# Residual of the last norm moved into the gate passes; factors for W2's first rows through the ring of f's blocks

## The chip, the cores and the metric

One core of a Trainium2 chip runs the whole layer in one launch. The metric is device time in microseconds, the median of several runs. Engines: PE (matmuls), DVE (vector), ACT (scalar, with activation functions), POOL and SP; SP, ACT and POOL also issue DMAs. Each engine runs its own instructions strictly in order.

## The reference

One layer of a transformer trunk in float32, with 512 tokens and 2048 features: two kinds of attention on one input projection, an output product, a layer norm, then a feed-forward part and a gated embedding, and a second layer norm:

```
mix = concat(RMSNorm_A(A), RMSNorm_B(B)) @ w_o
h   = LN1(alpha*x + mix)
ff  = square(relu(h @ w1)) @ w2                  # w1 2048 x 8192, w2 8192 x 2048
ple = (p @ w_ple) * sigmoid(h @ w_ple_gate)      # w_ple 256 x 2048, gate 2048 x 2048
out = LN2(alpha*h + ff + ple)                    # alpha = 2 ** 0.25
```

LN1 is `(x - mean) * rstd * ln1_g + ln1_b`, row by row. The term `alpha*h + ple` is what this text calls the residual.

## The kernel before

**Products.** From the output product on, every product is a call of `strassen`: two by two blocks, seven products in place of eight. A pass has 28 steps `(p, k)`, product p and row block k. A step loads a 128x1024 block of weights or makes a sum of such blocks on DVE, splits it into two parts for PE's fast float32 mode (`w_split`: `wh` on ACT, line 87, `wl = w - wh` on DVE, line 88; three buffers of each), and gives PE 12 matmuls of 128x512: `wh` with both parts of the activation's factor, `wl` with the first. Three chains of PSUM banks, `a`, `b` and `c`, hold the sums. After the last row block of a product, `read` copies or adds the chain into a tile of the ring `c` (line 682 on ACT, line 684 on DVE). `after` calls the consumer of a finished quarter two steps later.

**Order of the passes.** One pass of `w_o` by this method; two of the gate (c = 0, 1); eight of W1 (n = 0 to 7), each giving 1024 features of f; eight of W2 (m = 0 to 3, c = 0, 1). Between `w_o` and the gate, `norm_rows` normalises z, and `turned` (line 695) stores it to `z_d`, transposes it on PE, lets ACT apply LN1's gain and bias (line 708), and stores the result, h turned by features, to `h_d`. So `h_d` holds h itself, and `z_d` holds z without gain and bias.

**Factors.** The activation's factors, a high and a low part `s1h`/`s1l` to `s7h`/`s7l` for each half g, are made by `put` (ACT line 433, DVE line 434). For W2, `f_factors` loads blocks of f's sums from `s_d` (tile `qs`, line 589) and splits them, each at a step of the pass before, or, if its product is in `LATE`, at a step of the pass itself.

**Residual before.** In each gate pass `gated` (line 759) takes a sigmoid in place and stores it to `g_d`. In each W1 pass `residual(n % 2, n // 2)` has three parts, hung on steps 6, 10 and 13: `load` brings z, the sigmoid, the embedding's product and LN1's gain and bias, 512 KB each, through SP's queue; `scaled` (lines 778, 781) and `summed` (lines 786, 787) make the residual on DVE, and POOL's queue stores it back to `z_d`. W2's passes add to `z_d`, and the last ones read it.

**Rings.** `w_tile` gives buffers by tag, in turn: `r` 4 (weight blocks), `q` 2 (`wq`, and in f's factors `qs`), `k` 4, `c` 3, `g` 4 (the residual's tiles, h's blocks `qh`, and in W2 the weight blocks `wg` where `hold` is set). A tile that asks for a buffer waits until the former owner's last reader is done. A load that waits for its buffer holds the queue of the engine that issues it.

**Order of the instructions.** The program text gives priorities; the framework's scheduler settles the order on each engine when the kernel is built, and may move an instruction ahead of another one of its engine. What follows on the order is read from the built programs.

Of the kernel before, what the change touches and what calls it, by code (L numbers as in the profile page):

```python
# [11 lines left out]
F32 = mybir.dt.float32  # L12
# [26 lines left out]
def block_kernel(ctx: ExitStack, tc: tile.TileContext, xT, xn, pT, positions, w_in, w_o, w_gate, w_ple,  # L39
# [356 lines left out]

    g_d = dr.tile([2, 4, P, 2, S], F32, name="g_d")


    def embed(g, p, bank, pair_of):  # L400
# [180 lines left out]
    def f_factors(m, sg):  # L581


        at = {False: {}, True: {}}
        for p in range(1, 8):
            for g in range(2):
                def step(p=p, g=g):
                    x = block("qs", "q")
                    nc.sync.dma_start(x, s_d[2 * m + g, p - 1])
                    put(sg[g], p, x)  # L590
                late = p in LATE
                at[late].setdefault(LATE[p][g] if late else STEPS.index((p, 2 * g + 1)) + 2, []).append(step)
        return at
# [101 lines left out]
    def turned(th, n):  # L695

        z, g = zs[th, n], n % 2
        nc.gpsimd.dma_start(z_d[th, n], z)
        i = 2 * th + n // 2
# [58 lines left out]
    for c in range(2):  # L758
        def gated(th, nh, g, c=c):
            nc.scalar.activation(g, g, AF.Sigmoid)  # L760
            nc.scalar.dma_start(g_d[th, 2 * c + nh], g)
        strassen(lambda k, q, c=c: w_gate[c, q, k], sh, quarters(gated), between=mid if c == 0 else {},
                 steps=FIRST5 if c == 0 else None)

    def residual(th, n):

        t = {}

        def load():
            for name, d in (("zn", z_d), ("sg", g_d), ("pl", ple_d)):  # L770
                t[name] = pair(name, "g")
                nc.sync.dma_start(t[name], d[th, n])
            t["gb"] = pair("gb", "g")
            nc.sync.dma_start(t["gb"], bass.AP(tensor=lnb.tensor, offset=lnb.offset + n * S,
                                               ap=[[0, P], [D, 2], [1, S]]))

        def scaled():
            nc.vector.tensor_tensor(t["sg"], t["sg"], t["pl"], op=ALU.mult)
            for i in range(2):
                z = t["zn"][:, i]  # L780
                nc.vector.scalar_tensor_tensor(z, z, ALPHA, t["gb"][:, 0], op0=ALU.mult, op1=ALU.mult)

        def summed():
            for i in range(2):
                z = t["zn"][:, i]
                nc.vector.scalar_tensor_tensor(z, t["gb"][:, 1], ALPHA, z, op0=ALU.mult, op1=ALU.add)
            nc.vector.tensor_tensor(t["zn"], t["zn"], t["sg"], op=ALU.add)
            nc.gpsimd.dma_start(z_d[th, n], t["zn"])

        return load, scaled, summed  # L790

# [3 lines left out]
    for n in range(NFC):  # L795
        f = {}
        mid = dict(at[False]) if n == NFC - 1 else {}
        for i, step in zip((6, 10, 13), residual(n % 2, n // 2)):
            mid[i] = mid.get(i, []) + [step]

        def squared(th, nh, x, n=n, f=f):
# [16 lines left out]
            if (th, nh) == (0, 0):  # L818
# [5 lines left out]
                keep(3, f[0, 1])  # L824
        strassen(lambda k, q, n=n: w1[n, q, k], sh, quarters(squared), between=mid)

# [3 lines left out]
    def last_sum(c):  # L830
# [5 lines left out]
        def read(p, b):  # L836
# [11 lines left out]
            if c == 1 and p == 5:  # L848
                for n in range(2):
                    gb.append([])  # L850
                    for i in range(2):
                        x = s_tile("gb", ("s5h", "s5l")[i], (P, 1024))
                        off = lnb.offset + (2 + i) * D + n * 1024
                        nc.gpsimd.dma_start(x, bass.AP(tensor=lnb.tensor, offset=off, ap=[[0, P], [1, 1024]]))
                        gb[n].append(x)
# [144 lines left out]
```

## Time and profile before

| | us |
|---|---|
| median of 3 runs | 2275.27 (2273.86 to 2276.92) |
| profiled execution | 2280.34 |
| its span | 2278.6 |
| PE busy | 2166.3 (95%) |
| DVE busy | 1636.1 (72%) |
| ACT busy | 1060.7 (47%) |

Busy time adds up instructions of one engine; a busy PE says nothing on its clock, which the views of stretches give beside it as PEclk, 1.00 for full speed (2.4 GHz), and which falls to the lower level (1.2 GHz) for a while after idle time. The passes stand in this order in the span: `w_o` to about 704 us, the norm's turning to about 762, gate to 926 or so, W1 to about 1620, W2 to the end. In the views a wait is named by who ended it. DMA names read target<-source, so `gb<-in_lnb` is the load of LN1's gain and bias.

### The profile page before, as it was taken

How to read it: one execution, taken by the hardware profiler on the slowest of the kernel's cores; microseconds unless marked ns; L12 is line 12 of the kernel's file. 1: busy time of each engine (PE TensorE's matmuls, PEld its weight loads, DVE VectorE, ACT ScalarE, POOL GpSimd, SP SyncE). 2: the span in 40 equal slices, each digit the busy share in tenths (PEclk: the TensorE clock that was granted, in tenths of full speed). 3: DMA queues.
4: the chain of work that ended last, by engine and by line, in shares of the span. 5: the costliest groups of instructions: out<-in, count | busy, mean ns of one | idle time of the engine just before them, and what ended most of it. 6: DMA issues, size and time to landing. Idle time of an engine off the chain costs nothing.

```text
span 2278.6 us, 25699 instructions
## 1 busy us (share of the span) xinstructions
PE 2166.3 (95%) x9576; PEld 1752.2 (77%) x9576; DVE 1636.1 (72%) x1872; ACT 1060.7 (47%) x1287; POOL 115.1 (5%) x192
## 2 busy tenths in 40 slices
PE   8999999999997899999999999989999999999995
PEld 7888888877785688877778777776777787787784
DVE  7675655544878777776877877767767777777887
ACT  5454333343344554445445445455545555555331
POOL 0000000000001000000000000000011011011000
PEclk9999999999998999999999999999999999999998
DMA  6212322237566675566676676676778779679562
GB/s 228 75 65 84 116 72 82 78 113 261 167 211 234 241 244 196 169 229 205 221 239 208 219 238 204 220 257 228 247 208 261 195 196 290 178 209 291 181 242 102
DMA packets 133230, 438.79 MB, mean 193 GB/s; under 512 B 13776, under 2 KB 21984, under 8 KB 133104
## 3 DMA queue, kind: packets, MB, share of 16 engines
q1 hardware_dynamic: 98832, 316.45, 41.4%
q0 software_dynamic: 26336, 95.53, 14.6%
q10 hardware_dynamic: 7936, 25.17, 3.1%
q8 instruction: 75, 1.23, 0.2%
q14 instruction: 51, 0.42, 0.1%
HBM read 354.25 MB, written 82.84 MB: 192 GB/s over the span
## 4 chain that ended last, share of the span: by engine, by line
PE 66%; DMA 12%; issue 10%; DVE 10%; ACT 2%; POOL 0%; DVEq 0%; SPq 0%; ACTq 0%; POOLq 0%
PE a L666 8%; PE a L663 8%; PE a L665 8%; PE u L94 6%; PE u L96 6%; PE u L95 6%; DVE wl L88 4%; PE b L666 3%; PE b L663 3%; PE b L665 3%; DMA wr<-in_w 3%; PE c L666 3%; PE c L663 3%; PE c L665 3%; DMA s_d<-f 2%
## 5 line engine op out<-in xcount | busy, mean ns | idle before, releaser
L87 ACT ACTIVATE wh<-wr 128x1024 fp32r<-128x1024 f32 (+1 forms) x400 | 415.9, 1042 | 587.2 <-PE a L665 263.8
L88 DVE TENSOR_TENSOR wl<-wr,wh 128x1024 fp32r<-128x1024 f32 (+1 forms) x400 | 478.7, 1199 | 239.8 <-ACT wh L87 233.0
L87 ACT ACTIVATE wh<-wk 128x1024 fp32r<-128x1024 f32 x152 | 160.9, 1059 | 191.9 <-PE a L665 101.8
L94 PE MATMUL u<-xh,wh 128*128 128x512 f32 x576 | 227.4, 395 | 5.9 <-ACT xh L74 5.9
L96 PE MATMUL u<-xh,wl 128*128 128x512 f32 x576 | 225.7, 392 | 0.0
L88 DVE TENSOR_TENSOR wl<-wk,wh 128x1024 fp32r<-128x1024 f32 x152 | 185.1, 1221 | 56.4 <-ACT wh L87 56.3
L95 PE MATMUL u<-xl,wh 128*128 128x512 f32 x576 | 225.2, 391 | 0.0
L610 DVE TENSOR_TENSOR wk<-wr,wk 128x1024 f32<-128x1024 f32 x76 | 93.0, 1223 | 87.0 <-DMA wr<-in_w 78.0
L663 PE MATMUL b<-wh,s5h 128*128 128x512 f32 x304 | 122.4, 403 | 14.9 <-DVE c L684 8.4
L666 PE MATMUL a<-wl,s6h 128*128 128x512 f32 x304 | 122.0, 401 | 12.1 <-DVE wl L88 12.1
L94 PEld LDWEIGHTS u<-xh,wh 128*128 128x128 f32 x576 | 108.6, 188 | 27.6 <-ACT xh L74 5.9
L663 PE MATMUL a<-wh,s6h 128*128 128x512 f32 x304 | 121.7, 400 | 7.8 <-ACT ev L884 4.6
L96 PEld LDWEIGHTS u<-xh,wl 128*128 128x128 f32 x576 | 108.4, 188 | 22.8
L663 PE MATMUL a<-wh,s7h 128*128 128x512 f32 x304 | 120.6, 397 | 5.4 <-ACT wh L87 5.4
L95 PEld LDWEIGHTS u<-xl,wh 128*128 128x128 f32 x576 | 108.5, 188 | 22.3 <-DVE xl L75 0.4
L666 PE MATMUL b<-wl,s5h 128*128 128x512 f32 x304 | 122.5, 403 | 3.2 <-DVE wl L88 3.2
L665 PE MATMUL a<-wh,s1l 128*128 128x512 f32 x304 | 120.7, 397 | 4.7 <-DVE s1l L434 4.7
L666 PE MATMUL c<-wl,s2h 128*128 128x512 f32 x304 | 120.8, 397 | 3.7 <-DVE wl L88 3.6
L666 PE MATMUL a<-wl,s7h 128*128 128x512 f32 x304 | 120.5, 396 | 4.0 <-DVE wl L88 4.0
L666 PE MATMUL a<-wl,s1h 128*128 128x512 f32 x304 | 121.1, 398 | 2.0 <-DVE wl L88 2.0
L663 PE MATMUL a<-wh,s1h 128*128 128x512 f32 x304 | 121.2, 399 | 1.7 <-ACT wh L87 1.7
L663 PE MATMUL c<-wh,s2h 128*128 128x512 f32 x304 | 121.5, 400 | 0.3 <-ACT wh L87 0.3
(285 smaller groups left out, 4674.2 us busy)
## 6 DMA issues: line engine op xcount, KB each, us to landing
wr<-in_w SPq DMA_DIRECT2D x196, 512.0 KB, 4.4
wq<-in_w SPq DMA_DIRECT2D x72, 512.0 KB, 4.5
wr<-in_w_in SPq DMA_DIRECT2D x64, 512.0 KB, 3.8
wk<-in_w POOLq DMA_DIRECT2D x64, 512.0 KB, 5.5
qs<-s_d SPq DMA_DIRECT2D x56, 512.0 KB, 4.8
z_d<-ev POOLq DMA_DIRECT2D x42, 512.0 KB, 6.7
wr<-in_w_o SPq DMA_DIRECT2D x32, 512.0 KB, 4.3
s_d<-f POOLq DMA_DIRECT2D x32, 512.0 KB, 4.2
```

The lines of the kernel that those rows point to most:

```text
L87: nc.scalar.activation(hi, t, AF.Copy)
L88: nc.vector.tensor_tensor(lo, t, hi.bitcast(F32), op=ALU.subtract)
L94: nc.tensor.matmul(o, wh, ah, start=start, stop=False)
L95: nc.tensor.matmul(o, wh, al, start=False, stop=False)
L96: nc.tensor.matmul(o, wl, ah, start=False, stop=stop)
L610: nc.vector.tensor_tensor(t4[k], get(b21, k, 2, "r"), t2[k], op=ALU.subtract)
L663: nc.tensor.matmul(o, sh[:, i, x], wh[:, c], start=first and k == 0 and j == 0, stop=False, skip_group_check=skip)
L665: nc.tensor.matmul(o, sl[:, i, x], wh[:, c], start=False, stop=False, skip_group_check=skip)
L666: nc.tensor.matmul(o, sh[:, i, x], wl[:, c], start=False, stop=k == 3 and j == 1, skip_group_check=skip)
```

## The change

The residual is made in the gate passes. `gated` loads the embedding's product (`pl`) and a block of h turned by features (`hk`, from `h_d`) through ACT's queue into the ring `g`, multiplies sigmoid and product on DVE, transposes h back with eight transposes on PE, adds alpha times that out of PSUM on DVE (two instructions), and stores the sum to `z_d` from ACT's queue. With this `turned` no longer stores z, `residual` and `g_d` are gone, and W1's passes hold nothing of it. LN1's gain and bias are no longer among the inputs `lnb`. Second, the `qs` of W2's first rows (m = 0) take their buffers from `g` in place of `q`, and for the second half two of them, products 3 and 7, are split in the first W2 pass (steps 4 and 6) in place of the last W1 pass (steps 20 and 21).

```diff
--- before.py
+++ after.py
@@ -394,9 +394,6 @@
     hd.scores(q, k)
 
 
-    g_d = dr.tile([2, 4, P, 2, S], F32, name="g_d")
-
-
     def embed(g, p, bank, pair_of):
         wh, wl = w_split(w_load(w_ple[g], "r"))
         for th in range(2):
@@ -585,11 +582,12 @@
         for p in range(1, 8):
             for g in range(2):
                 def step(p=p, g=g):
-                    x = block("qs", "q")
+                    x = block("qs", "q" if m else "g")
                     nc.sync.dma_start(x, s_d[2 * m + g, p - 1])
                     put(sg[g], p, x)
-                late = p in LATE
-                at[late].setdefault(LATE[p][g] if late else STEPS.index((p, 2 * g + 1)) + 2, []).append(step)
+                plan = LATE if m or g == 0 else {**LATE, 3: (3, 4), 7: (3, 6)}
+                late = p in plan
+                at[late].setdefault(plan[p][g] if late else STEPS.index((p, 2 * g + 1)) + 2, []).append(step)
         return at
 
     def strassen(src, sg, read, hold=False, between={}, steps=None):
@@ -695,7 +693,6 @@
     def turned(th, n):
 
         z, g = zs[th, n], n % 2
-        nc.gpsimd.dma_start(z_d[th, n], z)
         i = 2 * th + n // 2
         ha[g, i] = x = s_tile("ha", {0: "s4h", 1: "s4l", 2: "s7h", 3: "s7l"}[i])
         for b0 in (0, 2):
@@ -757,47 +754,27 @@
     mid = {3 + 2 * n: [f] for n, f in enumerate(steps[0] + steps[1])}
     for c in range(2):
         def gated(th, nh, g, c=c):
+            n = 2 * c + nh
+            e = pair("pl", "g")
+            nc.scalar.dma_start(e, ple_d[th, n])
+            hk = block("hk")
+            nc.scalar.dma_start(hk, h_d[n % 2, 2 * th + n // 2])
             nc.scalar.activation(g, g, AF.Sigmoid)
-            nc.scalar.dma_start(g_d[th, 2 * c + nh], g)
+            nc.vector.tensor_tensor(g, g, e, op=ALU.mult)
+            for i in range(2):
+                pt = pt_bank()
+                for b in range(4):
+                    nc.tensor.transpose(pt[:, b * P:(b + 1) * P], hk[:, b, i * P:(i + 1) * P], ident)
+                nc.vector.scalar_tensor_tensor(g[:, i], pt, ALPHA, g[:, i], op0=ALU.mult, op1=ALU.add)
+            nc.scalar.dma_start(z_d[th, n], g)
         strassen(lambda k, q, c=c: w_gate[c, q, k], sh, quarters(gated), between=mid if c == 0 else {},
                  steps=FIRST5 if c == 0 else None)
-
-    def residual(th, n):
-
-        t = {}
-
-        def load():
-            for name, d in (("zn", z_d), ("sg", g_d), ("pl", ple_d)):
-                t[name] = pair(name, "g")
-                nc.sync.dma_start(t[name], d[th, n])
-            t["gb"] = pair("gb", "g")
-            nc.sync.dma_start(t["gb"], bass.AP(tensor=lnb.tensor, offset=lnb.offset + n * S,
-                                               ap=[[0, P], [D, 2], [1, S]]))
-
-        def scaled():
-            nc.vector.tensor_tensor(t["sg"], t["sg"], t["pl"], op=ALU.mult)
-            for i in range(2):
-                z = t["zn"][:, i]
-                nc.vector.scalar_tensor_tensor(z, z, ALPHA, t["gb"][:, 0], op0=ALU.mult, op1=ALU.mult)
-
-        def summed():
-            for i in range(2):
-                z = t["zn"][:, i]
-                nc.vector.scalar_tensor_tensor(z, t["gb"][:, 1], ALPHA, z, op0=ALU.mult, op1=ALU.add)
-            nc.vector.tensor_tensor(t["zn"], t["zn"], t["sg"], op=ALU.add)
-            nc.gpsimd.dma_start(z_d[th, n], t["zn"])
-
-        return load, scaled, summed
 
 
     sf = [{}, {}]
     at = f_factors(0, sf)
     for n in range(NFC):
         f = {}
-        mid = dict(at[False]) if n == NFC - 1 else {}
-        for i, step in zip((6, 10, 13), residual(n % 2, n // 2)):
-            mid[i] = mid.get(i, []) + [step]
-
         def squared(th, nh, x, n=n, f=f):
             f[th, nh] = y = block("f")
             for i in range(2):
@@ -822,7 +799,7 @@
                 keep(6, f[1, 1])
                 nc.vector.tensor_tensor(f[0, 1], f[0, 1], f[1, 1], op=ALU.subtract)
                 keep(3, f[0, 1])
-        strassen(lambda k, q, n=n: w1[n, q, k], sh, quarters(squared), between=mid)
+        strassen(lambda k, q, n=n: w1[n, q, k], sh, quarters(squared), between=at[False] if n == NFC - 1 else {})
 
 
     gb = []
@@ -850,7 +827,7 @@
                     gb.append([])
                     for i in range(2):
                         x = s_tile("gb", ("s5h", "s5l")[i], (P, 1024))
-                        off = lnb.offset + (2 + i) * D + n * 1024
+                        off = lnb.offset + i * D + n * 1024
                         nc.gpsimd.dma_start(x, bass.AP(tensor=lnb.tensor, offset=off, ap=[[0, P], [1, 1024]]))
                         gb[n].append(x)
         return read
@@ -981,7 +958,7 @@
         "w1": _quarters(a["w1"][0], halves),
         "w2": np.stack(w2),
         "vecs": vecs,
-        "lnb": np.stack([a[k][0] for k in ("ln1_g", "ln1_b", "ln2_g", "ln2_b")]),
+        "lnb": np.stack([a["ln2_g"][0], a["ln2_b"][0]]),
         "sink": a["sink_a"],
         "mask_a": ma,
         "mask_b": mb,
```

How the order moves, at three places.

DVE in the second W1 pass (n = 1), from the first step of product 6 on. Lines 778 to 787 are `residual`; line 615 is the sum of `sum3`, which takes two loaded blocks. Before:

```order
L778 TENSOR_TENSOR sg<-sg,pl 128x1024
L781 SCALAR_TENSOR_TENSOR zn<-zn,gb 128x512
L88 TENSOR_TENSOR wl<-wk,wh 128x1024
L781 SCALAR_TENSOR_TENSOR zn<-zn,gb 128x512
L615 TENSOR_TENSOR wq<-wr,wq 128x1024
L88 TENSOR_TENSOR wl<-wk,wh 128x1024
L786 SCALAR_TENSOR_TENSOR zn<-gb,zn 128x512 x2
L88 TENSOR_TENSOR wl<-wk,wh 128x1024
L787 TENSOR_TENSOR zn<-zn,sg 128x1024
L615 TENSOR_TENSOR wq<-wr,wq 128x1024
L88 TENSOR_TENSOR wl<-wr,wh 128x1024
```

The same place after; line 613 is the former line 615.

```order
L613 TENSOR_TENSOR wq<-wr,wq 128x1024 x2
L88 TENSOR_TENSOR wl<-wk,wh 128x1024 x3
L88 TENSOR_TENSOR wl<-wr,wh 128x1024
L88 TENSOR_TENSOR wl<-wq,wh 128x1024
L608 TENSOR_TENSOR wk<-wr,wk 128x1024
L88 TENSOR_TENSOR wl<-wr,wh 128x1024
```

Six kinds of instructions of `residual` are gone from between the `wl`, and the second sum of line 613 has moved ahead of the three `wl<-wk`.

DVE at the entry to the gate: `s1l` and `s2l` are low parts of h's factors 1 and 2, which the first gate pass waits for, `qh` is a block of h loaded back for factors 7, 3 and 4, and line 615 (613) belongs to a later step. Before:

```order
L434 TENSOR_TENSOR s2l<-ha,s2h 128x1024
L88 TENSOR_TENSOR wl<-wr,wh 128x1024 x2
L615 TENSOR_TENSOR wq<-wr,wq 128x1024
L434 TENSOR_TENSOR s1l<-ha,s1h 128x1024 x2
L88 TENSOR_TENSOR wl<-wr,wh 128x1024
```

After:

```order
L431 TENSOR_TENSOR s2l<-ha,s2h 128x1024
L625 TENSOR_TENSOR wq<-wq,wr 128x1024
L626 TENSOR_TENSOR wk<-wk,wq 128x1024
L88 TENSOR_TENSOR wl<-wq,wh 128x1024
L431 TENSOR_TENSOR s1l<-ha,s1h 128x1024 x2
L88 TENSOR_TENSOR wl<-wq,wh 128x1024
L567 TENSOR_TENSOR qh<-qh 128x1024
L88 TENSOR_TENSOR wl<-wr,wh 128x1024 x2
```

The sum of line 615 no longer stands ahead of `s1l`; a subtraction of two blocks `qh` (line 567) now stands ahead of two `wl`.

SP's queue in the last W1 pass, from the first of the `qs` that stand close together. Before:

```order
L589 DMA qs<-s_d 128x1024 x2
L80 DMA wr<-in_w 128x1024
L80 DMA wq<-in_w 128x1024
L589 DMA qs<-s_d 128x1024
L80 DMA wr<-in_w 128x1024
L80 DMA wq<-in_w 128x1024
L589 DMA qs<-s_d 128x1024
L80 DMA wr<-in_w 128x1024
L80 DMA wq<-in_w 128x1024
L589 DMA qs<-s_d 128x1024
```

After:

```order
L586 DMA qs<-s_d 128x1024
L80 DMA wr<-in_w 128x1024
L586 DMA qs<-s_d 128x1024 x4
L80 DMA wq<-in_w 128x1024
L586 DMA qs<-s_d 128x1024
L80 DMA wq<-in_w 128x1024
L586 DMA qs<-s_d 128x1024
L80 DMA wr<-in_w 128x1024 x2
L586 DMA qs<-s_d 128x1024
```

The `qs` now stand together ahead of the blocks `wq` of this pass's later steps; before, they took turns with them.

## Rows read from the trace of the kernel before

**Rows 1.** Page, part 1: busy time and instructions of each engine.

```profile
PE 2166.3 (95%) x9576; PEld 1752.2 (77%) x9576; DVE 1636.1 (72%) x1872; ACT 1060.7 (47%) x1287; POOL 115.1 (5%) x192
```

**Rows 2.** Busy time by stretch; columns in the first row.

```profile
core 0: us, PE busy (x) PEld busy (x) DVE busy (x) ACT busy (x) POOL busy (x), PEclk, DMA share, GB/s
...
772.00:848.70 76.70, 76.68 (x333) 61.92 (x332) 64.23 (x56) 42.19 (x41) 2.12 (x4) 1.00 0.66 224
848.70:926.05 77.35, 77.35 (x338) 63.03 (x337) 60.78 (x55) 37.28 (x37) 2.65 (x5) 1.00 0.63 211
926.05:1006.94 80.89, 80.89 (x370) 66.41 (x369) 57.83 (x50) 41.42 (x46) 4.25 (x8) 1.00 0.58 193
1006.94:1094.54 87.60, 82.99 (x370) 67.36 (x369) 64.09 (x58) 41.51 (x46) 4.79 (x9) 0.98 0.66 219
...
1436.40:1524.98 88.58, 82.31 (x367) 65.21 (x365) 61.95 (x56) 42.35 (x46) 4.79 (x9) 1.00 0.65 219
1524.98:1628.50 103.52, 90.89 (x379) 70.28 (x378) 78.44 (x70) 49.15 (x54) 4.79 (x9) 0.95 0.71 248
1628.50:1712.00 83.50, 79.61 (x329) 63.47 (x330) 58.22 (x50) 41.31 (x42) 8.36 (x11) 0.96 0.75 204
1712.00:1795.64 83.64, 80.55 (x338) 63.78 (x337) 65.30 (x58) 46.74 (x49) 8.28 (x11) 0.98 0.87 255
1795.64:1873.55 77.91, 77.83 (x338) 62.91 (x337) 53.01 (x46) 38.00 (x38) 8.26 (x11) 1.00 0.69 185
```

**Rows 3.** Waits, DVE and PE, 1007 to 1094: total, times, longest.

```profile
DVE zn L781 <- DMA gb<-in_lnb: 4.9, 1, 4.9
...
PE a L666 <- DVE wl L88: 3.3, 1, 3.3
```

**Rows 4.** Timeline of DVE at 1016: start, us, operation, [idle before].

```profile
1016.15 0.69 DVE L781 SCALAR_TENSOR_TENSOR zn<-zn,gb 128x512 f32<-128x512 f32 x1 [4.87 <-DMA gb<-in_lnb]
```

**Rows 5.** DVE groups by form: count, busy us, mean ns, idle before.

```profile
L781 DVE SCALAR_TENSOR_TENSOR zn<-zn,gb 128x512 f32<-128x512 f32 x16 | 10.9, 688 | 25.1 <-DMA gb<-in_lnb 23.3 <-issue 1.8
...
L778 DVE TENSOR_TENSOR sg<-sg,pl 128x1024 f32<-128x1024 f32 x8 | 9.8, 1224 | 6.5 <-DMA pl<-ple_d 6.5
...
L475 DVE SCALAR_TENSOR_TENSOR xt<-xt,u 128x512 f32<-128x512 f32 x8 | 5.3, 685 | 1.3 <-PE u L460 1.3
```

**Rows 6.** Waits of PE, 860 to 1560.

```profile
PE a L666 <- DVE wl L88: 14.0, 10, 3.3
```

**Rows 7.** Timeline of DVE, line 615 in the last W1 pass.

```profile
1551.56 1.23 DVE L615 TENSOR_TENSOR wq<-wr,wq 128x1024 f32<-128x1024 f32 x1 [2.55 <-DMA wq<-in_w]
...
1573.92 1.23 DVE L615 TENSOR_TENSOR wq<-wr,wq 128x1024 f32<-128x1024 f32 x1 [0.36 <-DMA wq<-in_w]
```

**Rows 8.** Timeline of ACT and PE in the first W2 pass.

```profile
1627.54 1.06 ACT L433 ACTIVATE s2h<-qs 128x1024 fp32r<-128x1024 f32 x1 [7.05 <-DMA qs<-s_d]
...
1629.56 0.50 PE L663 MATMUL a<-wh,s6h 128*128 128x512 f32 x1 [4.56 <-ACT ev L884]
...
1630.37 0.63 PE L663 MATMUL a<-wh,s6h 128*128 128x512 f32 x1
...
1633.78 0.40 PE L666 MATMUL a<-wl,s6h 128*128 128x512 f32 x1
```

**Rows 9.** Line 705's transposes, and PE's timeline around eight of them.

```profile
L705 PE MATMUL pt<-ident,xt x32: 271/273/329, 693.5 to 739.7; 128*128 128x128 f32 x32
...
693.55 1.33 PE L705 MATMUL pt<-ident,xt 128*128 128x128 f32 x8
694.63 0.48 PE L665 MATMUL b<-wh,s3l 128*128 128x512 f32 x1
```

**Rows 10.** Timeline of PE and DVE at the entry to the gate.

```profile
713.06 0.77 PE L663 MATMUL b<-wh,s5h 128*128 128x512 f32 x1 [8.45 <-DVE c L684]
...
760.09 1.22 DVE L615 TENSOR_TENSOR wq<-wr,wq 128x1024 f32<-128x1024 f32 x1 [5.13 <-DMA wr<-in_w_gate]
...
762.50 0.79 PE L665 MATMUL a<-wh,s1l 128*128 128x512 f32 x1 [4.73 <-DVE s1l L434]
```

## The prediction

> **What bounds the kernel now.** The page's first part comes first: PE is busy for 2166.3 us of the span [rows 1], so only some 112 us of idle time and the stretches at the lower clock can be won at all. Next I cut the span into passes. Every product of this half of the kernel is one call of `strassen` (28 steps of 12 matmuls), and the start of ACT's first copy out of chain `a` (line 682, in W2 line 884) marks the same point of each pass; busy time by stretch between these marks gives a table of passes [rows 2]. The reader is to compare like with like there. The two gate passes take 76.70 and 77.35 us with PE busy throughout. The first W1 pass takes 80.89, also with PE busy throughout. Of the six after it the first takes 87.60 and the last 88.58, and the stretch that holds the eighth pass takes 103.52. All do the same matmuls, so what lies above 80.89 is waiting, or clock lost by it.
>
> The view of waits says on what. In the second W1 pass DVE stands 4.9 us for the load of `gb`, and PE then 3.3 us for a `wl` that DVE owed it [rows 3]. The timeline shows the queue: line 781 of `residual` waits at the head of DVE, and the `wl` stands right behind it [rows 4]. Why is the first W1 pass clean? Because the scheduler put its residual (number 0) ahead of it, into the second gate pass, and what stands in 926.05 to 1006.94 holds none. Its 50 DVE instructions against 58 show that [rows 2]. So a pass without `residual` has already been timed inside this very run, and it runs at PE's pace.
>
> **W1 passes.** Taken out of each: two 128x1024 and four 128x512 vector operations, 2 x 1.22 + 4 x 0.69 = 5.2 us of DVE [rows 5], four loads of 512 KB from SP's queue and one store from POOL's. The six passes from 1006.94 to 1524.98 take 518.04; six times 80.89 is 485.34. The whole difference, 32.7 us, is the upper bound. The lower bound is what PE waited for `wl` behind the residual, 14.0 us over ten waits [rows 6]. I take 28, near the upper end, because the row of a pass without it is the nearest there can be; 4.7 are held back because the new order puts a second subtraction of line 613 (it waits for two weight loads) ahead of three `wl`, where the clean pass had one.
>
> **Last W1 pass and first W2 pass.** Together 103.52 + 83.50 = 187.02, against 80.89 and the 77.91 of a W2 pass that runs at PE's pace [rows 2]: 28.2 above it. Part is residual 7. Another part is the ring `q`: with two buffers, a block of f's factors (`qs`) and a W1 block (`wq`) take turns in it, so a `wq` is asked for only when the block before has been split. Line 615 starts at 1551.56 and, three turns on, at 1573.92, 7.45 us a turn of two steps [rows 7], while two steps at PE's pace take 2 x 77.35 / 28 = 5.5: four turns lose 7.7. The third part is a `qs` that came late: ACT stood 7.05 us for it, and the copy of chain `a` behind it made PE wait 4.56 [rows 8]. In the ring `g` the `qs` are issued four ahead and the `wq` have both buffers of `q`. What comes late next is DVE: a pass with ten such splits takes 83.64, one with four takes 77.91, thus 5.7 for ten [rows 2]. The last W1 pass will hold eight and the first W2 pass six, two of them moved there by the new plan. I let 7 us stay and take 21 off. Bounds: 28 (all of it) and 8 (the turns alone).
>
> **Gate passes.** Added: eight calls of `gated`, each with 8 transposes on PE, and on DVE one product of 1.22 and two sums out of PSUM, for which the nearest row is line 475 with 0.69 [rows 5]. PE has no slack here, so the transposes count in full. A W1 pass differs from a gate pass on PE by its 32 transposes: 80.89 - 77.35 = 3.54, or 0.11 each, so 64 cost 7.1. From start to start eight of them took 1.08 [rows 9], which makes 8.6.
>
> The Trainium skill speaks against the change here ("TensorE: Matmul & The Clock Gate", Part 4: PE-mode transpose): about 275 ns for a transpose in a kernel, and transposes don't count as activity for the clock. The duration agrees with the row, 273 ns [rows 9], but they overlap, and the pass with 32 of them ran at a granted clock of 1.00 [rows 2]. By that rule 64 x 0.275 = 17.6 us would be lost in place of 7.1, near the third rival below.
>
> DVE's 2.6 us a call make 10.4 a pass. The first gate pass goes from 64.23 busy to 74.6 of 80 us, the second, rid of residual 0, from 60.78 to 66. Its `wl` are made up to three steps ahead (three buffers), that is 8 us of cover for a call. Where DVE had 65.30 in a W2 pass, 5.7 were lost [rows 2]; here nothing that DVE multiplies is loaded late, since the four buffers of `g` let `pl` and `hk` be issued a call ahead, so I add 2 for both passes: +9 in all. Bounds +7 (transposes alone) and +20 (both passes lose as that W2 pass does, and the transposes cost 8.6). The loads and the store stand in ACT's queue ahead of `wh`; that the store of `g` stood there before at no cost to PE is in the same two rows.
>
> **Entry to the gate.** No line was meant for it, but the order changes. Before, a subtraction of line 615 stood ahead of the last two splits of h's factor 1 on DVE; it waited 5.13 us for a weight block, and PE stood 4.73 for that factor [rows 10]. Now those splits come first. The eight stores of z ahead of h's stores in POOL's queue go too. Against it, the first subtraction of `factors`, which waits for two loads of h, now stands ahead of the next two `wl`. I take -5 (the wait that goes). Bounds: -13 (the 8.45 us wait at 713.06 goes as well [rows 10]) and +5 (the new wait for h is as long as the old one).
>
> **Sum.** -28 - 21 + 9 - 5 = -45 us. The profiled execution took 2280.3 us (span 2278.6 and 1.7 around it), so it would take 2235; it lies 5.1 over the median of the runs, 2275.3, so the prediction is 2230. Bounds added: -33 - 28 + 7 - 13 = -67, or 2208; and -14 - 8 + 20 + 5 = +3, or 2278.
>
> **Rivals.**
> First, only the waits that carry `residual`'s own name go: the later `wr` waits of the W1 passes stay, DVE still bounds the last one, nothing is won at the entry. -14 - 8 + 9 = -13, or 2262. For it: DVE stays busy for some 58 of 81 us in a pass. Against it: the clean pass had the same load.
> Second, slower: ACT's queue. In `gated` two loads and a store stand between the `wh` of the gate steps, and each can hold ACT until a buffer of `g` comes free or DVE is done. The price of one such hold is in the trace: 4.56 us of PE, and then eight matmuls at the lower clock from 1630.37 to 1633.78, 0.43 each in place of 0.23, 6.2 in all [rows 8]. The gains of 54 are gone at (54 - 7) / 6.2 = 7.6 holds, about one a call; with twelve of 24 it is 7 + 74 - 54 = +27, or 2302. Against it: PE lost nothing in the gate passes with eight stores in that place.
> Third, the transposes don't overlap and each costs its whole row, 64 x 0.273 = 17.5 in place of 7.1 [rows 9]: -45 + 10.4 = -34.6, or 2241, on the same side as the forecast. Against it: eight in a row took 1.08 and not 2.2.
> Fourth, the entry and the gate give back what W1 wins (h loaded late, and some four holds): about 2275, no change.
>
> **How the numbers follow.** Forecast (2208 to 2252) 0.70, first rival 0.13, third 0.07, second 0.06, fourth 0.04. A change of 0.2%, 4.6 us, is about what these measurements can tell from none. Faster by more than that: 0.70 + 0.13 + 0.07 = 0.90; within it 0.04; slower 0.06. The range runs from the lower bound to part of the first rival: 2207 to 2258.
>
> **What would show it.** Right: W1 passes of 81 to 82 us each, from mark to mark, with no DVE wait for a load of line 774's kind; the last W1 and first W2 pass together near 166; gate passes near 81 at clock 1.00; no 5 us wait for factor 1. Wrong: waits of ACT ahead of `wh` in the gate passes and PE idle behind them, DVE waiting on `pl` or `hk`, W1 passes that stay above 84 (then the load of `gb` was not the cause), or line 615 still 7 us apart in the last W1 pass.

## The result and the profile after

The changed kernel takes 2237.22 us (median of 4 runs, 2234.28 to 2241.54), the kernel before 2276.1 beside it (4 runs, 2273.86 to 2278.74): ratio 0.983, with a 95% interval of 0.9811 to 0.985. The profiled executions stand at 2234.28 and 2280.34, 46.1 apart, where the medians are 38.9 apart.

Page, part 1, of the kernel after, against [rows 1]: 15.9 us less of PE's busy time in spite of 64 more instructions, and 18.1 less of DVE's.

```profile
PE 2150.4 (96%) x9640; PEld 1752.3 (78%) x9640; DVE 1618.0 (72%) x1848; ACT 1060.7 (48%) x1287; POOL 105.8 (5%) x176
```

Busy time by stretch, after, between the same marks as in [rows 2] (start of ACT's first copy out of chain `a`): two gate passes, the W1 passes 0, 1, 2, 6 and 7, two W2 passes.

```profile
core 0: us, PE busy (x) PEld busy (x) DVE busy (x) ACT busy (x) POOL busy (x), PEclk, DMA share, GB/s
770.75:847.34 76.59, 76.55 (x352) 62.52 (x351) 67.23 (x64) 38.27 (x38) 2.12 (x4) 1.00 0.79 269
847.34:926.82 79.48, 79.48 (x360) 65.09 (x359) 63.74 (x59) 36.21 (x36) 2.11 (x4) 1.00 0.61 212
926.82:1008.51 81.69, 81.69 (x373) 67.06 (x372) 60.76 (x53) 42.36 (x46) 4.25 (x8) 1.00 0.61 202
1008.51:1089.40 80.89, 80.89 (x370) 66.41 (x369) 59.69 (x52) 41.40 (x46) 4.25 (x8) 1.00 0.60 200
1089.40:1170.29 80.89, 80.89 (x370) 66.42 (x369) 59.69 (x52) 41.39 (x45) 4.26 (x8) 1.00 0.62 204
...
1413.31:1497.59 84.28, 82.29 (x373) 66.93 (x372) 60.13 (x52) 43.19 (x47) 4.26 (x8) 1.00 0.63 204
1497.59:1582.09 84.50, 82.22 (x367) 66.08 (x366) 68.79 (x61) 48.63 (x53) 4.26 (x8) 0.99 0.72 249
1582.09:1660.87 78.78, 78.17 (x337) 63.37 (x336) 60.55 (x53) 41.68 (x43) 8.31 (x11) 0.99 0.82 239
1660.87:1743.84 82.97, 80.04 (x338) 63.88 (x337) 63.70 (x56) 46.66 (x49) 8.30 (x11) 0.98 0.86 252
```

One correction to the table of before: its first row starts at 772.00, which is not a mark. From mark to mark the first gate pass of before, a shorter one, is this row, and 76.59 is to be compared with it:

```profile
777.20:848.70 71.50, 71.48 (x310) 57.69 (x309) 59.03 (x52) 38.39 (x38) 2.12 (x4) 1.00 0.68 230
```

So the account by stretches of the two profiled executions reads:

| from mark to mark, us | before | after | difference | predicted |
|---|---|---|---|---|
| `w_o` to the first gate pass | 136.93 | 132.59 | -4.3 | -5 |
| two gate passes and W1 pass 0 | 229.74 | 237.76 | +8.0 | +9 |
| W1 passes 1 to 6 | 518.04 | 489.08 | -29.0 | -28 |
| W1 pass 7 and the first W2 pass | 187.02 | 163.28 | -23.7 | -21 |

All else comes to +2.7: -2.1 ahead of `w_o`'s mark, 0.0 over the next four W2 passes, and +4.8 from the last mark (that of the sixth W2 pass) to the end of the span. From that mark on PE, DVE and ACT carry out the same instructions in the same order in all fourteen profiles (before, after and the twelve kernels below), and the end took 246.7 to 250.0 us in the twelve, 249.6 after and 244.8 before: scatter from execution to execution.

PE's waits, after, in the stretch that held ten waits for `wl` before [rows 6]; columns are total, times, longest.

```profile
PE b L664 <- DVE wl L88: 1.8, 1, 1.8
```

One is left. Four of the six W1 passes lie at PE's pace, as the clean pass of before did, and a fifth takes 81.23. The one wait ends at 1496.11, in pass 6, which lasts 84.28. It has another cause, shown by ACT's and then DVE's timeline (start, us, operation, [idle before]): a block of f for W2's factors lands late, ACT waits for it, DVE for ACT, and the `wl` stands behind.

```profile
1491.46 1.06 ACT L430 ACTIVATE s1h<-qs 128x1024 fp32r<-128x1024 f32 x1 [5.37 <-DMA qs<-s_d]
```

```profile
1492.56 1.23 DVE L431 TENSOR_TENSOR s1l<-qs,s1h 128x1024 fp32r<-128x1024 f32 x1 [2.31 <-ACT s1h L430]
```

### The profile page after: what moved, and what is told of

The parts are those of the page before. It is cut to its first block, busy times and chain, and to the rows that moved or that the text cites. A ratio compares the mean times of both kernels' runs of the same rounds, so it can differ in the third digit from the quotient of the medians.

```text
span 2232.2 us, 25725 instructions
## 1 busy us (share of the span) xinstructions
PE 2150.4 (96%) x9640; PEld 1752.3 (78%) x9640; DVE 1618.0 (72%) x1848; ACT 1060.7 (48%) x1287; POOL 105.8 (5%) x176
## 4 chain that ended last, share of the span: by engine, by line
PE 81%; DVE 7%; DMA 7%; issue 2%; ACT 1%; DVEq 0%; SPq 0%; ACTq 0%
PE a L664 11%; PE a L661 11%; PE a L663 11%; PE u L94 6%; PE u L95 6%; PE u L96 6%; PE b L664 5%; PE b L663 5%; PE b L661 5%; DMA wr<-in_w 3%; DVE wl L88 3%; PE c L664 3%; PE c L663 3%; PE c L661 3%; PE pt L783 1%
## 5 line engine op out<-in xcount | busy, mean ns | idle before, releaser
L96 PEld LDWEIGHTS u<-xh,wl 128*128 128x128 f32 x576 | 108.6, 188 | 22.8
L661 PE MATMUL a<-wh,s4h 128*128 128x512 f32 x304 | 120.8, 397 | 0.7 <-DVE zl L815 0.7
L663 PE MATMUL b<-wh,s3l 128*128 128x512 f32 x304 | 121.3, 399 | 0.0
L664 PE MATMUL b<-wl,s3h 128*128 128x512 f32 x304 | 120.0, 395 | 1.3 <-DVE wl L88 1.0
L663 PE MATMUL c<-wh,s2l 128*128 128x512 f32 x304 | 121.2, 399 | 0.0
L663 PE MATMUL a<-wh,s4l 128*128 128x512 f32 x304 | 120.4, 396 | 0.0
```

The costliest lines, as they stand in the source:

```text
L96: nc.tensor.matmul(o, wl, ah, start=False, stop=stop)
L661: nc.tensor.matmul(o, sh[:, i, x], wh[:, c], start=first and k == 0 and j == 0, stop=False, skip_group_check=skip)
L663: nc.tensor.matmul(o, sl[:, i, x], wh[:, c], start=False, stop=False, skip_group_check=skip)
L664: nc.tensor.matmul(o, sh[:, i, x], wl[:, c], start=False, stop=k == 3 and j == 1, skip_group_check=skip)
```

## The experiments

Medians carry their ratio to the kernel before, run on the same chip; "six passes" are W1 passes 1 to 6, from mark to mark, in the profiled execution (518.04 before, 489.08 after).

### W1: is it the load, DVE's work, or both?

**Only the load of `gb` taken from the kernel before.**

```diff
-            t["gb"] = pair("gb", "g")
-            nc.sync.dma_start(t["gb"], bass.AP(...))
-                nc.vector.scalar_tensor_tensor(z, z, ALPHA, t["gb"][:, 0], ...)
+                nc.vector.scalar_tensor_tensor(z, z, ALPHA, t["pl"][:, i], ...)
```

> The kernel before without the load of LN1's gain and bias (gb), the fourth load of each residual; DVE keeps its six instructions, two of its operands are taken from pl instead (so the residual's values differ). Theory (the late load is what cost: DVE stands for gb, and the wl behind it makes PE wait): the six W1 passes from 1006.94 on, 518.0 us before, fall to 490 to 500; PE's waits for wl between 860 and 1560 fall from 14.0 to under 5; total 2247 to 2257. Rival (5.2 us of DVE work in each pass, whose wl come late whatever the loads do): the six stay at 508 or more, total 2266 or more. Between them: another load (pl) becomes the late one, 500 to 508.

Measured: 2247.46 (2245.6 to 2248.29, 4 runs), ratio 0.9878 (0.9856 to 0.99). Six passes 496.37; the next two 177.31. DVE's instructions are all there, and 21.7 of the 29 us are gone. PE's waits in the six passes:

```profile
PE pt L803 <- DVE c L684: 5.3, 4, 2.9
PE b L663 <- ACT wh L87: 2.6, 1, 2.6
PE a L666 <- DVE wl L88: 0.2, 1, 0.2
```

Those for `wl` fell to 0.2, and to 1.6 over the whole stretch of [rows 6], where they were 14.0. The 2.9 is pass 1, still 86.02 long: a `wr` landed 3.9 us late, and this time DVE's sum of chain `c` (line 684) stood behind it. The theory holds for most of the gain, not for all.

**Only the DVE work put back into the kernel after.**

```diff
+        def first(t=t):
+            t["x"] = pair("dum", "g")
+            nc.gpsimd.memset(t["x"], 0.0)
+        # steps 10 and 13: the six DVE instructions on t["x"]
```

> The kernel after with the residual's six DVE instructions back in every W1 pass at the same steps, on a tile of the ring g that POOL fills with zeros, with no load and no store. Theory (waits for loads): six W1 passes, 489.1 us after, grow by 0 to 6; total 2237 to 2246. Rival (DVE time): 4 to 5 us in each, six passes at 513 to 518, total 2270 to 2280.

Measured: 2235.18 (2233.11 to 2237.32, 4 runs), ratio 0.9825 (0.9802 to 0.9849). Six passes 491.01, that is +1.9; the total lies 2 us below the range that I gave. In six kernels below that leave this part as it is, with DVE's order there the same as after, the six passes took 488.6 to 489.4, so the 1.9 is more than scatter, but little. DVE's time alone costs next to nothing; that rival falls.

**Only the loads put back.**

```diff
+            for d in (z_d, ple_d, ple_d, z_d):
+                nc.sync.dma_start(pair("dum", "g"), d[th, c])
```

> The kernel after with four loads of 512 KB from SP's queue into the ring g at step 6 of every W1 pass, as before, which nothing reads. Theory (the load was late for DVE's residual, and only that instruction carried the wait to PE): with no reader the six W1 passes stay within 489 to 495; total 2237 to 2246. Rival (the loads hold SP's queue for a buffer of g, so the weight blocks behind them come late, or the traffic of the DMAs does it): each pass 2 to 5 us longer, six at 501 to 518, total 2253 to 2275, with DVE waiting for wr or wk in place of gb.

Measured: 2240.31 (2237.62 to 2242.17, 4 runs), ratio 0.9844 (0.9817 to 0.9871). Six passes 494.30, +5.2, at the upper end of what I gave the theory. Part of the rival is true: DVE's waits over the six passes show that the weight blocks come later behind loads that wait for a buffer. With the loads, and then in the kernel after:

```profile
DVE wq L613 <- DMA wq<-in_w: 28.0, 13, 4.6
```

```profile
DVE wq L613 <- DMA wq<-in_w: 5.4, 10, 0.7
```

This points to the queue and not to the traffic: `wq` took a median of 4.1 us from issue to landing, against 4.0 after, while SP stood 55.6 us in front of the dead loads (line 805), which come ahead of the weight blocks in its queue. SP's waits in the six passes:

```profile
SPq L805 <- DMA s_d<-f: 35.3, 7, 6.2
SPq L805 <- DMA dum<-z_d: 20.3, 6, 4.0
```

**Both: the whole old residual as dead work beside the new one.**

```diff
+        for i, step in zip((6, 10, 13), residual(n % 2, n // 2)):
+            mid[i] = mid.get(i, []) + [step]
+            # residual as before; its store goes to a scratch array
```

> The kernel after with the whole of the old residual put back into the W1 passes as dead work beside the new one: four loads (the last one gb, 512 KB), the six DVE instructions that read them, the store into a scratch array that nothing reads. Theory (the loads alone gave back 5 us of the six passes and the DVE instructions alone 2; the other 20 come only when a DVE instruction reads the late load, with the wl queued behind it): the six W1 passes at 510 to 520 against 489.1, total 2258 to 2272, DVE waiting for gb in each pass. Rival (the two costs only add): 494 to 498, total 2243 to 2248.

Measured: 2261.93 (2261.07 to 2268.82, 7 runs), ratio 0.995 (0.9935 to 0.9965). Six passes 516.10. DVE's and PE's waits from 1009 to 1526:

```profile
DVE zn L792 <- DMA gb<-in_lnb: 14.8, 5, 3.6
```

```profile
PE a L664 <- DVE wl L88: 9.0, 6, 2.6
PE pt L813 <- DVE c L682: 8.5, 6, 2.0
```

The wait for `gb` is back, in five passes and not in each of the six. The loads cost 5.2, the work 1.9, both together 27.0: about 20 us are the price of a DVE instruction that reads a late load with `wl` and sums of `c` queued behind it. This run also has the residual's store, which the two runs before it lack. The store is not the price: the kernel without `gb` has it, with the six DVE instructions and three loads, and its six passes lie 7.3 above those of after.

### Last W1 pass and first W2 pass: ring or residual?

**The second part of the change undone.**

```diff
-                    x = block("qs", "q" if m else "g")
+                    x = block("qs", "q")
-                plan = LATE if m or g == 0 else {**LATE, 3: (3, 4), 7: (3, 6)}
+                plan = LATE
```

> The kernel after with its second part undone: the qs of m = 0 take their buffers from the ring q again, and products 3 and 7 of the second half are split in the last W1 pass as before. Theory (the gain in the last W1 and first W2 pass is two gains: the residual's, which the kernel before without gb bounds at 187.0 - 177.3 = 9.7 or somewhat more, and the ring's): the two passes, 163.3 us after, take 170 to 177, with the line of sum3 seven us a turn apart again; the other passes as after; total 2244 to 2252. Rival (residual 7 was the whole of it): 162 to 167, total within 4 us of after's 2237.

Measured: 2243.95 (2238.28 to 2244.99, 4 runs), ratio 0.987 (0.9853 to 0.9888). The two passes take 94.99 + 80.36 = 175.35. DVE's timeline of line 613 there:

```profile
1518.28 1.22 DVE L613 TENSOR_TENSOR wq<-wr,wq 128x1024 f32<-128x1024 f32 x1 [1.30 <-DMA wq<-in_w]
...
1525.56 1.23 DVE L613 TENSOR_TENSOR wq<-wr,wq 128x1024 f32<-128x1024 f32 x1 [0.18 <-DMA wq<-in_w]
...
1532.78 1.22 DVE L613 TENSOR_TENSOR wq<-wr,wq 128x1024 f32<-128x1024 f32 x1 [0.16 <-DMA wq<-in_w]
...
1539.99 1.23 DVE L613 TENSOR_TENSOR wq<-wr,wq 128x1024 f32<-128x1024 f32 x1 [0.17 <-DMA wq<-in_w]
```

And in the kernel after:

```profile
1504.72 2.35 DVE L613 TENSOR_TENSOR wq<-wr,wq 128x1024 f32<-128x1024 f32 x2
...
1518.54 1.22 DVE L613 TENSOR_TENSOR wq<-wr,wq 128x1024 f32<-128x1024 f32 x1
...
1522.17 1.23 DVE L613 TENSOR_TENSOR wq<-wr,wq 128x1024 f32<-128x1024 f32 x1
```

7.2 us a turn is close to the 7.45 of [rows 7], with no residual in the pass: two buffers that `wq` and `qs` share make it. The late `qs` of [rows 8] is back as well: ACT stood 5.1 us for one, and PE then 2.6 us for the copy behind it:

```profile
PE a L661 <- ACT ev L861: 2.6, 1, 2.6
```

**The ring kept, the old plan of splits.**

```diff
-                plan = LATE if m or g == 0 else {**LATE, 3: (3, 4), 7: (3, 6)}
+                plan = LATE
```

> The kernel after with the ring g for the qs but the old plan of splits (ten on DVE in the last W1 pass instead of eight). Theory (the ring is most of the second part's gain, the plan a small rest, 0.57 us a split by the W2 passes of before): 164 to 168 for the two passes against 163.3, total 2237 to 2242. Rival 1 (the plan does all): 170 to 177, as with the ring q. Rival 2 (ten splits in a pass cost 5.7 us there, as in the second W2 pass of before): 168 to 170.

Measured: 2232.29 (2226.76 to 2235.76, 4 runs), ratio 0.9822 (0.9801 to 0.9842). The two passes 85.74 + 78.82 = 164.56, +1.3. The total lies below the range that I gave. In six kernels below, whose order of instructions here is that of after, the two passes took 162.8 to 166.1, so the plan's 1.3 can't be told from nothing, here or in the total. Of the 23.7 us, the residual gave 11.7 (187.02 to 175.35), the ring 10.8 (to 164.56), each known to some 3 us by that scatter.

### The gate: what do the 8 us consist of?

**Without the transposes.**

```diff
-                pt = pt_bank()
-                for b in range(4):
-                    nc.tensor.transpose(pt[:, b * P:(b + 1) * P], hk[...], ident)
-                nc.vector.scalar_tensor_tensor(g[:, i], pt, ALPHA, g[:, i], ...)
+                nc.vector.scalar_tensor_tensor(g[:, i], hk[...], ALPHA, g[:, i], ...)
```

> The kernel after without the 64 transposes in the gate passes: the two sums of gated read the block of h as it lies in SBUF, not turned (so the residual's values differ); loads, DVE's instructions and the store stay. Theory (the 8.0 us that the gate passes and the pass behind them grew are PE's time for the transposes and nothing else, 0.125 each): the three stretches, 76.6, 79.5 and 81.7 after, go back to 71.5, 77.4 and 80.9 within 0.5 each; total 2227 to 2232. Rival 1 (part of the 8 is ACT's queue or DVE): under 5 us come back. Rival 2 (the transposes slow the matmuls around them as well, by their own overhead): over 9 come back.

Measured: 2234.17 (2234.11 to 2237.37, 4 runs), ratio 0.9836 (0.9821 to 0.985). The theory failed: the three stretches take 74.16 + 83.18 + 80.89 = 238.23 against 237.76, so nothing came back. A wait took the place of the transposes. PE's timeline near the end of the second gate pass, with the first matmul at the lower clock behind it, and DVE's ahead of that `wl`:

```profile
912.76 0.40 PE L663 MATMUL a<-wh,s1l 128*128 128x512 f32 x1
915.95 0.58 PE L664 MATMUL b<-wl,s5h 128*128 128x512 f32 x1 [2.79 <-DVE wl L88]
916.34 0.63 PE L661 MATMUL b<-wh,s5h 128*128 128x512 f32 x1
```

```profile
911.21 1.22 DVE L763 TENSOR_TENSOR c<-c,pl 128x1024 f32<-128x1024 f32 x1
912.35 1.22 DVE L626 TENSOR_TENSOR wk<-wk,wr 128x1024 f32<-128x1024 f32 x1
913.48 1.28 DVE L765 SCALAR_TENSOR_TENSOR c<-hk,c 128x512 f32<-128x512 f32 x2
914.69 2.35 DVE L88 TENSOR_TENSOR wl<-wr,wh 128x1024 fp32r<-128x1024 f32 x2
```

DVE is busy without a pause from 903.19 to 917, and `gated`'s product and sums stand ahead of the `wl`. This pass holds 5.8 of the 8.5 us by which the three stretches exceed before's 229.74. But the order on DVE is not that of the kernel after, where a `wl` stands between the product and the sums of the same call:

```profile
913.20 1.22 DVE L763 TENSOR_TENSOR c<-c,pl 128x1024 f32<-128x1024 f32 x1
914.33 1.22 DVE L88 TENSOR_TENSOR wl<-wr,wh 128x1024 fp32r<-128x1024 f32 x1
915.47 1.28 DVE L768 SCALAR_TENSOR_TENSOR c<-pt,c 128x512 f32<-128x512 f32 x2
```

Without the transposes, line 626 and the sums come ahead of the next `wl`, 2.3 us of DVE (912.35 to 914.69) against a wait of 2.8. So it is not shown how much of the wait is DVE's added work and how much is the order that the scheduler chose once the transposes were gone.

**Every transpose twice.**

```diff
-                for b in range(4):
+                for b in 2 * list(range(4)):
```

> The kernel after with every transpose of the gate passes issued twice into the same place (128 instead of 64). Without the transposes the three stretches of the gate took 238.2 us, and with them 237.8, so their removal gave nothing: a wl came late instead. Theory (PE's 8 us and DVE's work lie side by side: without the transposes DVE is late, with them it has cover; PE is the bound with them): the second 64 count in full, three stretches at 245 to 247, no PE idle. Rival (the transposes lie in time that PE would wait anyway): 238 to 241.

Measured: 2240.09 (one run); the three stretches 80.59 + 84.39 + 80.89 = 245.87, +8.1. Their first two:

```profile
771.40:851.99 80.59, 80.55 (x383) 66.34 (x382) 68.35 (x65) 38.39 (x38) 2.13 (x4) 1.00 0.73 255
851.99:936.38 84.39, 83.70 (x397) 68.72 (x396) 65.65 (x62) 37.16 (x38) 2.12 (x4) 1.00 0.61 208
```

PE is idle for 0.7 us, where I had said none, and its clock is 1.00. With the first 64 in place, PE is the bound, and 64 more cost 0.127 each, or 0.116 without the idle time.

**The transposes without `gated`'s DVE work.**

```diff
-            nc.vector.tensor_tensor(g, g, e, op=ALU.mult)
-                nc.vector.scalar_tensor_tensor(g[:, i], pt, ALPHA, g[:, i], ...)
```

> The kernel after with the loads and transposes of the gate passes but without the three DVE instructions of gated (the residual is left out: the sigmoid alone is stored). Theory (the 64 transposes alone cost PE 8 us, DVE's part nothing while they are there): the three stretches at 237 to 238.5, as with everything. Rival (the 8 us are DVE's, as the run without transposes could also be read): 229.7 to 233.

Measured: 2241.57 (one run); the three stretches 79.32 + 81.44 + 80.89 = 241.65. Neither expectation is met, since the experiment brought a wait of its own. With no reader of `pl`, a buffer of `g` can come round again before its load has landed, and ACT, which issues the next load into it, waits with its `wh` behind. ACT's timeline, and PE's behind the second of these holds:

```profile
821.45 1.06 ACT L87 ACTIVATE wh<-wr 128x1024 fp32r<-128x1024 f32 x1 [3.27 <-DMA pl<-ple_d]
...
842.29 1.06 ACT L87 ACTIVATE wh<-wr 128x1024 fp32r<-128x1024 f32 x1 [2.91 <-DMA pl<-ple_d]
...
847.12 1.06 ACT L87 ACTIVATE wh<-wk 128x1024 fp32r<-128x1024 f32 x1 [3.77 <-DMA pl<-ple_d]
```

```profile
846.48 0.50 PE L664 MATMUL a<-wl,s1h 128*128 128x512 f32 x1 [2.09 <-DVE wl L88]
```

So the first gate pass does not measure the transposes alone. The second does: it holds 32 of them, nothing of `gated` on DVE, no idle time of PE, and a clock of 1.00.

```profile
850.95:932.39 81.44, 81.44 (x372) 66.81 (x371) 56.69 (x49) 37.27 (x37) 2.11 (x4) 1.00 0.57 188
```

Against the 77.35 of [rows 2], which has no idle time either, the transposes cost 4.1, or 0.13 each (0.11 when two more matmuls that fall into this stretch are taken off at 0.23). Twice that is the 8 us of the theory. And the mechanism of the prediction's second rival exists: three holds of 10.0 us in all, and one that reached PE.

**The loads of `pl` and `hk` in SP's queue.**

```diff
-            nc.scalar.dma_start(e, ple_d[th, n])
+            nc.sync.dma_start(e, ple_d[th, n])
```

> The kernel after with the loads of pl and hk in SP's queue instead of ACT's. Theory (neither queue is held, since the four buffers of g come free a call ahead; nobody waits for these loads): the two gate passes stay within 1 us of 76.6 and 79.5, total 2235 to 2241. Rival (a load that waits for its buffer of g holds the weight blocks behind it in SP's queue): 3 to 10 us more in each gate pass, DVE or ACT waiting for wr, wq or wk, total 2243 to 2257.

Measured: 2235.47 (2232.37 to 2238.35, 4 runs), ratio 0.9833 (0.9816 to 0.9851); gate passes 75.89 + 80.08 = 155.97 against 156.07. For the loads either queue will do; the stores stayed in ACT's.

### The entry: order or scatter? And a faster kernel

**The eight stores of z put back,** with which DVE's order there is that of before.

```diff
+        nc.gpsimd.dma_start(g_d[th, n], z)
```

> The kernel after with turned's eight stores of z put back (into a scratch array that nothing reads); DVE's order at the entry to the gate is then that of before. Theory (the entry gained by its order: line 615's sum stood ahead of s1l and waited for a weight block): the stretch from w_o's mark to the first gate pass's mark, 132.6 us after and 136.9 before, goes back to 135.5 to 138, with PE waiting 4 to 5 us for s1l. Rival (it is the scatter of DMA times between two executions, or the stores' traffic and not the order): 131.5 to 134.

Measured: 2236.56 (one run); from mark to mark 136.70. PE's and DVE's waits in it (line numbers are two higher than after):

```profile
PE a L665 <- DVE s1l L433: 4.1, 1, 4.1
```

```profile
DVE wq L615 <- DMA wr<-in_w_gate: 4.5, 1, 4.5
```

The pair of waits of [rows 10] is back with the order, and 4.1 us with it. It is not scatter: this stretch took 135.5 to 136.9 in the three profiles with these stores (before, before without `gb`, and this one), and 131.0 to 134.0 in ten without them (after and nine of the kernels above). The stores bring their traffic and the old order together, so no run tells these two apart. The total doesn't show the 4 us; one run can't.

**Work that waits for nothing, moved into the entry's waits.**

```diff
+        if th == 0 and (th, 5 - n) in zs:        # ahead of the last half's norm
+            for g in range(2, 4):
+                embed(g, rest[0], pt_bank, lambda th: s_tile("pe", ...))
-    for g in range(2, 4):
-        embed(g, rest[0], pt_bank, lambda th: pair("pe", "g"))
```

> The kernel after with the last two embedding products called ahead of the last half's norm instead of behind it (their results in other tiles of the same memory), so that their 48 matmuls stand on PE right behind w_o's last step, where PE waits 8.0 us for the last sum of chain c and 7.0 us for a wl of the first gate step. Theory (the entry's 15 us of waits are DVE's chain of sum, norm and split, and work that depends on none of it fills them): from w_o's mark to the first gate mark 122 to 128 in place of 132.6, total 2226 to 2232, ratio to before 0.979 to 0.981. Rival 1 (the embedding's own splits lengthen DVE's chain by as much): 131 to 134, total 2235 to 2240. Rival 2 (the norm is put off and the first gate pass starts later): 135 to 142, total over 2240.

Measured: 2224.06 (2219.07 to 2228.92, 5 runs), ratio 0.9783 (0.9757 to 0.9808), 2 us below the range I gave; nothing of the layer is left out. From mark to mark the entry takes 123.95, 8.6 less than after. PE's longest waits at the entry, after, and then with the move:

```profile
PE b L661 <- DVE c L682: 8.0, 1, 8.0
PE b L664 <- DVE wl L88: 7.0, 1, 7.0
```

```profile
PE b L661 <- DVE c L682: 7.7, 1, 7.7
PE b L661 <- ACT wh L87: 4.0, 1, 4.0
PE pt L95 <- DVE wl L88: 2.2, 1, 2.2
```

The 7.0 for the first gate step's `wl` is gone, and the embedding's matmuls stand where it was; PE is idle for 15.6 us of the stretch, 23.0 after. The two kernels' intervals against before stand apart by a hair (0.9808 and 0.9811), and they were not run beside each other. The profile's 8.6 at the place of the edit is the better evidence. The two profiled spans differ by only 5.2, since the last W1 and first W2 pass, whose order did not change, took 2.5 longer here.

## Why the prediction was right, point by point

**W1 passes: right, 29.0 for 28, but the cause is two things.** I had put all of it on the residual's waits. The load of `gb` alone explains 21.7 of 29; dead loads with no reader cost 5.2, by holding weight blocks back in SP's queue; DVE's work alone costs 1.9. The costs don't add: only a late load together with a reader in DVE's order makes most of the loss. The 4.7 that I held back for line 613's second sum ahead of three `wl` did not come as I said (four of the six passes lie at 80.89 or 80.90); 3.4 came in pass 6, with the wait behind a late block of f.

**Last W1 and first W2 pass: right, 23.7 for 21.** I let 7 us stay; 163.28 is 4.5 above 80.89 and 77.91. The turns were the lower bound, 7.7, and the ring measured 10.8; with the ring `q` put back, PE's wait behind a late `qs` came back too, at 2.6. The two splits that the plan moves I had at 0.57 each, 1.1 together, by reading the two rows of [rows 2] as 5.7 for ten splits. That reading is off: from mark to mark the two stretches hold 13 and 1 of line 434, so it is 5.7 for twelve, 0.48 each. 1.3 was measured, too small to be told from scatter.

**Gate: +8.0 for +9, with one step wrong.** The transposes cost what a W1 pass's cost before, and the term of 2 for DVE did not come. Of the 8.0, some 1.2 are no cost at all: ahead of the first gate mark PE has done 407 matmuls since `w_o`'s mark, transposes not counted, where it had done 412 before, so five more fall into these stretches (5 x 0.23, an estimate). What is left is 6.9, or 0.11 for each transpose, as I had said. In the run with the stores put back, whose first mark stands as before, the three stretches take 237.02, +7.3. The DVE load that I gave for the first gate pass, 74.6 us, was too high, since it came from the row that starts at 772.00; from mark to mark DVE went from 59.03 to 67.23.

What I had wrong is that the two parts add. The transposes alone cost 4.1 in the pass that shows them cleanly, about half of 8; DVE's part alone cost 8.5 over the three stretches; both together cost 8.0. So they do not add, but why is shown in part only. My reading is that PE's 8 us are DVE's cover. The run without the transposes doesn't prove it, as DVE's order changed with them.

The 273 ns of the transposes' row [rows 9] are not what one costs: 64 added 8.0 us and 64 more 8.1, at a granted clock of 1.00. The Trainium skill ("TensorE: Matmul & The Clock Gate", Part 4: PE-mode transpose) gives about 275 ns for one of 128x128 in bf16 in one kernel's context; as a duration the row agrees (here in float32), as a price in a row of eight among matmuls the runs make it less than half. An estimate by its figure, 64 x 0.275 = 17.6 against 8.0, would have put the kernel at 2237 + 9.6 = 2247.

**Entry: -4.3 for -5, but not by less waiting.** The new wait for two loads of h, the bound of +5, did not come: DVE stood 1.7 us ahead of that subtraction. The wait of [rows 10] for factor 1 went, as said. But what I did not foresee is a 7.0 us wait of PE for the first gate step's `wl`, behind the embedding's splits and the norm; and the 8.45 us wait whose end made the bound of -13 is still there with 8.0. The stretch before and after, columns as in [rows 2]:

```profile
640.27:777.20 136.93, 114.17 (x478) 87.91 (x477) 102.55 (x126) 68.80 (x91) 11.40 (x20) 0.90 0.67 233
638.16:770.75 132.59, 109.54 (x473) 85.72 (x472) 101.74 (x126) 68.53 (x90) 6.38 (x12) 0.90 0.62 212
```

PE's idle time did not fall (22.8 and 23.0 us). Its busy time fell, by 4.6: five matmuls fewer lie between the marks, 1.2 by the estimate above, and by the timeline 18 matmuls run at the lower clock's pace where 34 did, 16 x (0.43 - 0.23) = 3.2 by an estimate from the paces of [rows 8]. So "the wait that goes" was paid for by another wait, and that the sum came out near -5 is in part luck.

**The sum, and where 7 us were lost.** The terms sum to -45; in the profiled pair the four stretches gave -49.0, and with all else the executions lie 46.1 apart. The predicted median is 2230 and the measured one 2237.22, inside the forecast's own range. The step that missed is the last, "it lies 5.1 over the median of the runs, so the prediction is 2230": it took the same offset off the changed kernel, whose profiled execution (2234.28) turned out the fastest of its four, 2.9 below their median, while that of before lay above its own. So the pair of profiles overstates the gain by 7. Whether part of the 5.1 was in the waits that the change removed stays open; one profile of before can't tell.

**Rivals.** That only the waits with `residual`'s own name go falls with the first row of the second pass, 80.89. ACT's queue cost PE nothing in the gate, and for the loads the run with SP's queue says the same; but ACT was held: once its `wh` stood 3.1 us behind a store that waited for DVE's sum,

```profile
ACT wh L87 <- DVE c L768: 3.1, 1, 3.1
```

while PE was busy for 76.55 of 76.59 and 79.48 of 79.48 us. The transposes at their full row fall with the doubled ones. The fourth, that the entry and the gate give back what W1 wins, falls with -4.3 and +8.0.

## What to carry to other kernels

Look for a pass of the same program that happens to lack the work in question: its row is a measured forecast, and its 80.89 us are what four of the six passes then took, within 0.01. An instruction that reads a late load costs by what is queued behind it, so take away the reader or the load; the two alone cost a quarter of what they cost together. Where two engines are nearly level, the costs of an addition to both need not add, and its removal from one of them may give nothing back, all the more as it can change the order on the other.

## What had not been expected of the hardware

- Taking 8 us of PE's work out gave nothing (237.8 to 238.2 us): a `wl` then came 2.8 us late, and the matmuls behind it ran at the lower clock (0.63 us for 0.39). Part of this may be DVE's changed order.
- A load that nothing reads can stall its issuer: three waits of ACT of 2.9 to 3.8 us for `pl` when a buffer was used again.
- The same instructions in the same order at the end of the program took between 244.8 and 250.0 us over fourteen profiles, a spread as large as the smallest terms of the sum; one pair of profiles can't settle a term of that size.
